# Gates, branch, output and down projections of an encoder layer in token-major form

## The chip, the core and the metric

One Trainium2 chip, one of its cores. The core has five engines with a queue each: TensorE (PE, with its weight loads shown as PEld), VectorE (DVE), ScalarE (ACT), GpSimd (POOL) and SyncE (SP), which here issues the transfers. The metric is device time of one execution in microseconds.

## What is computed

One layer for 256 tokens, `D_MODEL` 2048, all in float32. Cut to what the change touches:

```python
proj = h @ w_in                       # ..., the last 3 * 2048 columns are the gates
y_lru, y_attn, y_mem = ...            # recurrence, windowed attention, memory attention
gates = sigmoid(gl + b_gate).reshape(B, S, 3, D_MODEL)
merged = (gates[:, :, 0] * (y_lru @ w_br_lru) + gates[:, :, 1] * (y_attn @ w_br_attn)
          + gates[:, :, 2] * (y_mem @ w_br_mem))
x = x + rmsnorm(merged @ w_out, norm_mix_post)
hm = rmsnorm(x, norm_mlp_pre)
u = square(relu(hm @ w_up))           # 8192 wide
x = x + rmsnorm(u @ w_down, norm_mlp_post)
```

## The kernel before

Every product is float32 made of three fp32r products: a value is split into a high part (`h`, a rounded copy made by ACT) and a low part (the rest, made by DVE), and high x high, high x low and low x high are summed in PSUM. Weights come from DRAM as 344 chunks of 1 MB, each in two halves. `part` (line 106) issues a half's transfer on SP, lets ACT make `wh` and DVE make `wl`; `ahead` does this for the next chunk after each chunk's matmuls and then runs one step of every waiting list (`later`, `tick`). Five raw halves and four split halves have buffers. A scheduler sets the final order within each engine's queue; each queue runs in that order.

There are two forms of a product. In the **feature-major** form (`proj`, line 143) a chunk holds 128 output features for all 2048 inputs: the weights are the stationary operand, and the activations, high and low side by side, move: 16 matmuls of 512 columns with `wh` and 16 of 256 with `wl`. The result has 128 features on the partitions and its two halves are added on the way out (`ysum`, line 211: ACT copies one half, DVE adds the other, POOL multiplies by the norm's factor where one is given). `proj_one` (line 178) does the same with 48 matmuls of 256 columns into one half; `quad` (line 155) takes four chunks cut along the inputs and makes four results at once, so that it can begin when the first activations are there. In the **token-major** form (`proj_tok`, line 195) four chunks cut along the inputs make 512 features for two halves of 128 tokens: the activations are stationary and the weights move, 24 matmuls of 512 columns a chunk, and the result has tokens on the partitions. Before, this form serves the values of both attentions only.

The stages in order: the recurrence in four groups (`lru_group`), each with `quad` or `proj_one` chunks and, in the first three, gate chunks of the first branch behind it; keys, values and queries of the attention; the last gates, then the three branch products (`branch`, line 842) with the next gates or the memory attention between them; w_out; the norm, the residual `x1` and the split `h2` of the normed residual; `quad` for the first four w_up results; w_up and w_down in turn, four times. Gates get the norm's factor from POOL and bias and sigmoid from ACT; a branch result is multiplied and added by POOL. After w_out, squares are summed by POOL over the feature tiles, and `rstd_now` (line 358) sums over the partitions with small matmuls, takes the root, and spreads the factor over the partitions with another matmul; `warm` issues ten matmuls whose result nobody reads. All elementwise pages come from one pool of 31 pages of 4 KB for a partition.

## Time and profile before

| | us |
|---|---|
| median of three runs | 2093.64 (2091.84 to 2093.82) |
| profiled execution | 2091.72 |
| its span | 2089.9 |
| TensorE busy in it | 2032.9 |
| VectorE, ScalarE, GpSimd busy | 1358.2, 1081.8, 574.0 |

The span is from the first to the last instruction of the program; the execution's own time is 1.8 us longer. TensorE's matmuls overlap, so a matmul's length is longer than the distance to the next one: distances of starts tell the pace.

### The profile page before, as it was taken

The numbers are of one execution on the slowest core, as the hardware profiler recorded it, in microseconds if no ns is written. First come the engines' busy times: TensorE is split into PE (matmuls) and PEld (weight loads), VectorE is DVE, ScalarE is ACT, GpSimd is POOL, SyncE is SP. The second block draws the span as 40 slices with busy tenths as digits, with TensorE's granted clock in tenths as the row PEclk, the third lists the DMA queues.
The fourth block names the chain that finished last, engine by engine and source line by source line (L and its number), as shares of the span: only waits on it lengthen the run. The fifth ranks groups of instructions, "written<-read, shape, count | busy, mean of one in ns | idle before, by whom it ended". The sixth has DMA issues, their size and how long they took to land. (4 is left out here: it accounts for less than half of the span.)

```text
span 2089.9 us, 31160 instructions
## 1 busy us (share of the span) xinstructions
PE 2032.9 (97%) x12092; PEld 1811.8 (87%) x12092; DVE 1358.2 (65%) x1687; ACT 1081.8 (52%) x1607; POOL 574.0 (27%) x538
## 2 busy tenths in 40 slices
PE   8999999899999999999999999989999999999996
PEld 7999889799888888888888888878888888888886
DVE  8986685887557665555655555686556556555665
ACT  5877767567445454444454444444444444444442
POOL 5224141641116431000102237721001111111176
PEclk9999999999999999999999999999999999999998
DMA  6554546454566655555555556345555655556552
GB/s 228 189 184 148 190 157 201 152 169 144 183 196 206 202 187 176 181 172 175 179 171 183 190 199 218 128 165 188 192 189 184 194 189 186 195 184 191 191 187 96
DMA packets 108613, 378.25 MB, mean 181 GB/s; under 512 B 12720, under 2 KB 16816, under 8 KB 108464
## 3 DMA queue, kind: packets, MB, share of 16 engines
q1 hardware_dynamic: 108464, 376.26, 54.6%
q8 instruction: 94, 1.54, 0.3%
q14 instruction: 55, 0.45, 0.1%
HBM read 371.49 MB, written 2.10 MB: 179 GB/s over the span
## 5 line engine op out<-in xcount | busy, mean ns | idle before, releaser
L113 DVE TENSOR_TENSOR wl<-raw,wh 128x1024 fp32r<-128x1024 f32 (+1 forms) x691 | 897.1, 1301 | 234.8 <-ACT wh L112 228.1
L112 ACT ACTIVATE wh<-raw 128x1024 fp32r<-128x1024 f32 (+1 forms) x691 | 723.2, 1050 | 156.3 <-PE ps L137 58.6
L213 ACT ACTIVATE evac<-ps 128x256 f32<-128x256 f32 x294 | 112.2, 383 | 577.4 <-PE ps L137 574.1
L137 PE MATMUL ps<-hm,wh 128*128 128x512 f32 x1344 | 336.3, 393 | 0.0
L137 PEld LDWEIGHTS ps<-hm,wh 128*128 128x128 f32 x1344 | 244.6, 189 | 45.1
L137 PE MATMUL ps<-u,wh 128*128 128x512 f32 x1008 | 241.1, 391 | 0.0
L137 PE MATMUL ps<-h,wh 128*128 128x512 f32 x960 | 229.9, 391 | 0.0
L137 PEld LDWEIGHTS ps<-u,wh 128*128 128x128 f32 x1008 | 185.3, 188 | 35.8
L137 PEld LDWEIGHTS ps<-h,wh 128*128 128x128 f32 x960 | 176.4, 188 | 34.2
L141 PEld LDWEIGHTS ps<-hm,wl 128*128 128x128 f32 x1344 | 173.1, 192 | 12.0 <-DVE wl L113 5.4
L141 PE MATMUL ps<-hm,wl 128*128 128x256 f32 x1344 | 175.4, 283 | 5.2 <-DVE wl L113 5.2
L216 POOL TENSOR_TENSOR y<-y,rstd 128x256 f32<-128x256 f32 x64 | 49.1, 768 | 393.5 <-DVE y L214 372.9
L214 DVE TENSOR_TENSOR y<-ps,evac 128x256 f32<-128x256 f32 x111 | 47.0, 424 | 157.1 <-ACT evac L213 157.1
L189 PE MATMUL ps<-hm,wl 128*128 128x256 f32 x448 | 129.4, 289 | 11.9 <-DVE wl L113 11.9
L141 PEld LDWEIGHTS ps<-u,wl 128*128 128x128 f32 x1008 | 129.3, 191 | 4.9
L141 PE MATMUL ps<-u,wl 128*128 128x256 f32 x1008 | 130.8, 283 | 0.0
L187 PE MATMUL ps<-hm,wh 128*128 128x256 f32 x448 | 128.4, 287 | 1.0 <-ACT wh L112 1.0
L188 PE MATMUL ps<-hm,wh 128*128 128x256 f32 x448 | 128.0, 286 | 0.0
L141 PEld LDWEIGHTS ps<-h,wl 128*128 128x128 f32 x960 | 123.1, 191 | 4.7
L141 PE MATMUL ps<-h,wl 128*128 128x256 f32 x960 | 124.5, 283 | 0.0
L216 POOL TENSOR_TENSOR gate<-gate,rstd 128x256 f32<-128x256 f32 x48 | 43.0, 896 | 248.5 <-DVE gate L214 233.0
L189 PEld LDWEIGHTS ps<-hm,wl 128*128 128x128 f32 x448 | 87.3, 195 | 13.8 <-DVE wl L113 13.8
(283 smaller groups left out, 3084.5 us busy)
## 6 DMA issues: line engine op xcount, KB each, us to landing
raw<-wall SPq DMA_DIRECT2D x687, 512.0 KB, 3.5
raw<-wgate SPq DMA_DIRECT2D x8, 512.0 KB, 4.3
swap<-ry SPq DMA_DIRECT2D x40, 64.0 KB, 2.4
mp<-memT SPq DMA_DIRECT2D x4, 512.0 KB, 4.9
x<-xT SPq DMA_DIRECT2D x4, 512.0 KB, 4.6
xp<-xT SPq DMA_DIRECT2D x7, 256.0 KB, 6.9
out<-x SPq DMA_DIRECT2D x6, 256.0 KB, 2.3
raw<-wall SPq DMA_DIRECT2D x4, 128.0 KB, 2.5
```

The source lines that it names most:

```text
L112: nc.scalar.activation(hi[:, s], raw[:, s], AF.Copy)
L113: nc.vector.tensor_tensor(lo[:, s], raw[:, s], hi[:, s].bitcast(F32), op=ALU.subtract)
L137: self.nc.tensor.matmul(ps, wh, act[k // 2][:, k % 2, :], start=(k == 0), stop=(k == KT - 1))
L141: self.nc.tensor.matmul(ps[:, S:], wl, act[k // 2][:, k % 2, :S], start=False, stop=False)
L187: nc.tensor.matmul(o, wh, a[:, :S], start=(k == 0), stop=False)
L188: nc.tensor.matmul(o, wh, a[:, S:], start=False, stop=False)
L189: nc.tensor.matmul(o, wl, a[:, :S], start=False, stop=(k == KT - 1))
L213: self.nc.scalar.activation(t, ps[:, S:2 * S], AF.Copy)
L214: self.nc.vector.tensor_tensor(out, ps[:, :S], t, op=ALU.add)
L216: self.nc.gpsimd.tensor_tensor(out, out, r, op=ALU.mult)
```

## The change

The gates, the three branches, w_out and w_down now use the token-major form, so `merged`, `z`, `x1` and `z2` hold tokens on the partitions, four tiles of 512 features. `tok_mms` is the new inner part of `proj_tok`, which goes through half a chunk at a time: first all matmuls with `wh`, then those with `wl`. `proj_tok_late` does the last group of w_out and of w_down: its last two chunks run for the first 128 tokens, then for the second 128, and `after` is called for each. The norm's factor is one number for each partition now: ACT squares with a sum along the row (`squares`), `token_rstd` adds four sums, takes root and reciprocal, and the factor goes into one DVE operation with the residual (`scalar_tensor_tensor`). Gate biases and post-norm gains come as rows copied to all partitions. `w_up` stays feature-major, so the merged rows and the residual are transposed by TensorE (`turned`, `feed`): eight groups of four 128x128 transposes each. `feed` stands inside `quad`, two pairs of input tiles ahead. `rxcol`, the factor for each token, is made in the first group. `warm` behind w_out is gone. The attention's mask and its identity are fp32r tiles instead of bf16.

```diff
-    def proj_tok(self, act, specs):
...
-                for t in range(2):
-                    xh = a[:, t * P:(t + 1) * P]
-                    xl = a[:, S + t * P:S + (t + 1) * P]
-                    nc.tensor.matmul(pst[t], xh, wh, start=(k == 0), stop=False)
-                    nc.tensor.matmul(pst[t], xh, wl, start=False, stop=False)
-                    nc.tensor.matmul(pst[t], xl, wh, start=False, stop=(k == KT - 1))
+    def tok_mms(self, pst, act, ci, w, ts):
...
+        for half in range(2):
...
+            for i, k in enumerate(ks):
+                for t in ts:
+                    xh, xl = xs[k, t]
+                    nc.tensor.matmul(pst[t], xh, wh[i], start=(k == 0), stop=False)
+                    nc.tensor.matmul(pst[t], xl, wh[i], start=False, stop=False)
+            for i, k in enumerate(ks):
+                for t in ts:
+                    nc.tensor.matmul(pst[t], xs[k, t][0], wl[i], start=False, stop=(k == KT - 1))
+    def proj_tok_late(self, act, specs, after):
...
+        pair = [self.chunk(spec) for spec in specs[2:]]
+        for t in range(2):
+            for i in range(2):
+                self.tok_mms(pst, act, 2 + i, pair[i], (t,))
+            if t:
+                self.ahead()
+            after(t, pst[t])
+    def token_rstd(self, ssq):
...
+        tot = self.small.tile([P, 1], F32, tag="tot", name="tot")
+        nc.vector.reduce_sum(tot, ssq, axis=AX.X)
+        nc.scalar.activation(tot, tot, AF.Sqrt, scale=1.0 / D, bias=self.eps[:, 0:1])
+        nc.vector.reciprocal(tot, tot)
...
+    def squares(self, src, acc):
+        junk = self.tmp.tile([P, 2, S], F32, tag="pr", name="junk", bufs=3)
+        self.nc.scalar.activation(junk.rearrange("p a b -> p (a b)"), src, AF.Square, accum_out=acc)
+    def transposed(self, srcs, base):
...
+        tp = self.psc.tile([P, 2, S], F32, tag="sc", name="ft")
+        for t in range(2):
+            for kt in range(2):
+                at = base + kt * P
+                nc.tensor.transpose(tp[:, kt, t * P:(t + 1) * P], srcs[t][:, at:at + P], self.ident)
...
-                nc.tensor.matmul(far, self.identb, self.masks[t], start=False, stop=False)
+                nc.tensor.matmul(far, self.identr, self.masks[t], start=False, stop=False)
@@ gates_ahead @@
-                    self.gate(j, n, hm, held[n])
+            b = self.bias_tile(j, n)
+            pst = self.proj_tok(hm, [("T", "w_in", 9216 + j * D + n * 512, c) for c in range(4)])
...
+            for t in range(2):
+                nc.vector.scalar_tensor_tensor(g[:, t, :], pst[t], self.rxcol[:, t:t + 1], b, op0=ALU.mult, op1=ALU.add)
@@ branch @@
-        ps = self.proj(y, ("F", wname, n * P))
...
-        self.ysum(ps, t)
...
-            nc.gpsimd.tensor_tensor(t, t, g, op=ALU.mult)
-            nc.gpsimd.tensor_tensor(out, t, prev, op=ALU.add)
+        pst = self.proj_tok(y, [("T", wname, n * 512, c) for c in range(4)])
+        for t in range(2):
+            nc.vector.tensor_tensor(g[:, t, :], pst[t], g[:, t, :], op=ALU.mult)
+        if total is not None:
+            nc.vector.tensor_tensor(total, total, g, op=ALU.add)
@@ run, w_out to w_up @@
-                ps = self.proj(mg, ("F", "w_out", n * P))
-                self.ysum(ps, o)
-                self.square_into(acc, o, n == 0)
-                nc.gpsimd.tensor_scalar(o, o, gcol, None, op0=ALU.mult)
...
-        rp, r = self.rstd_now([acc, last])
-        self.warm(10)
+                self.squares(ps, ssq[:, t, n:n + 1])
+                nc.vector.tensor_tensor(z[n][:, t, :], ps, gains[n // 2][:, n % 2, :], op=ALU.mult)
...
+        def last_z(t, ps):
+            z_done(3)(t, ps)
...
+            rows.append(self.token_rstd(ssq[:, t, :]))
+            if t == 0:
+                for n in range(4):
+                    x1_part(0, rows[0], n, slice(0, 512))
...
+        def feed(p):
...
+            n, i = divmod(p, 2)
+            x1_part(1, rows[1], n, slice(2 * i * P, 2 * (i + 1) * P))
+            tp = self.transposed([x1[n][:, t, :] for t in range(2)], 2 * i * P)
...
+            for k in (2 * p, 2 * p + 1):
+                self.scaled_split(tp[:, k % 2, :], self.v("norm_mlp_pre", k), *self.hl(h2, k))
...
+        ups = self.quad(h2, [("T", "w_up", 0, c) for c in range(4)], feed)
@@ run, w_down @@
-                    self.ysum(self.proj(u, ("D", q, n * P)), t)
-                    nc.gpsimd.tensor_tensor(o, o, t, op=ALU.add)
...
+                        nc.vector.tensor_tensor(o, ps, o, op=ALU.add)
...
+                        self.squares(o, ssq[:, t, n:n + 1])
+                        nc.vector.tensor_tensor(o, o, gains[n // 2][:, n % 2, :], op=ALU.mult)
...
+            def last_z2(t, ps):
+                z2_done(3)(t, ps)
...
+                r = self.token_rstd(ssq[:, t, :])
+                for n in range(4):
...
+                    nc.vector.scalar_tensor_tensor(x, o, r, x, op0=ALU.mult, op1=ALU.add)
+                    nc.sync.dma_start(self.io["out"][:, t, n * 512:(n + 1) * 512], x)
```

What this does to the order, at three places. **TensorE, from the last w_up chunk to the first w_down chunk.** `ps` and `pst` are PSUM results, `h2` the normed residual, `u` the squared activations, `wh` and `wl` the weights' parts; numbers count tiles. Before:

```order
L137 MATMUL ps_14194<-h2_13358,wh_14179 128x512 x2
L137 MATMUL ps_14248<-u_13577,wh_14227 128x512 x2
L137 MATMUL ps_14248<-u_13594,wh_14227 128x512 x2
L137 MATMUL ps_14248<-u_13656,wh_14227 128x512 x2
L137 MATMUL ps_14248<-u_13763,wh_14227 128x512 x2
L141 MATMUL ps_14248<-u_13577,wl_14228 128x256 x2
L141 MATMUL ps_14248<-u_13594,wl_14228 128x256 x2
```

Now:

```order
L139 MATMUL ps_12770<-h2_12037,wh_12755 128x512 x2
L207 MATMUL pst_12824<-wh_12803,u_12153 128x512
L208 MATMUL pst_12824<-wh_12803,u_12153 128x512
L207 MATMUL pst_12825<-wh_12803,u_12153 128x512
L208 MATMUL pst_12825<-wh_12803,u_12153 128x512
L207 MATMUL pst_12824<-wh_12803,u_12153 128x512
L208 MATMUL pst_12824<-wh_12803,u_12153 128x512
L207 MATMUL pst_12825<-wh_12803,u_12153 128x512
L208 MATMUL pst_12825<-wh_12803,u_12153 128x512
L211 MATMUL pst_12824<-wl_12804,u_12153 128x512
L211 MATMUL pst_12825<-wl_12804,u_12153 128x512
L211 MATMUL pst_12824<-wl_12804,u_12153 128x512
```

The w_down chunk had 16 matmuls of 512 columns and 16 of 256; half a chunk now has eight with `wh` and four with `wl`, all of 512 and two of them for each token half and input tile.

**VectorE, from the norm behind w_out into `quad`.** `wl` are weight parts for w_up, `x` the residual, `h` the low part of the normed residual. Before:

```order
L113 TENSOR_TENSOR wl<-raw,wh 128x1024 x3
L933 TENSOR_SCALAR z<-ps,vec 128x256
L367 RECIPROCAL rcol<-rcol 128x2
L371 TENSOR_SCALAR diag<-ident,rcol 128x128 x2
L948 TENSOR_TENSOR z<-z,rb 128x256 x2
L949 TENSOR_TENSOR x_12421<-x_12421,z 128x256 x2
L952 TENSOR_TENSOR x_12421<-x_12421,z 128x512
L412 SCALAR_TENSOR_TENSOR h_13301<-x_12421,vec,h_13301 128x256 x2
...
L412 SCALAR_TENSOR_TENSOR h_13358<-x_13052,vec,h_13358 128x256 x2
L113 TENSOR_TENSOR wl<-raw,wh 128x1024 x4
```

Now:

```order
L965 SCALAR_TENSOR_TENSOR x_11679<-z,tot,x_11679 128x512
L115 TENSOR_TENSOR wl<-raw,wh 128x1024
L961 TENSOR_TENSOR z<-pst,gain 128x512
L385 TENSOR_REDUCE tot<-ssq 128x1
L115 TENSOR_TENSOR wl<-raw,wh 128x1024
L387 RECIPROCAL tot<-tot 128x1
L115 TENSOR_TENSOR wl<-raw,wh 128x1024
L965 SCALAR_TENSOR_TENSOR x_11198<-z,tot,x_11198 128x256 x2
L965 SCALAR_TENSOR_TENSOR x_11369<-z,tot,x_11369 128x256 x2
L965 SCALAR_TENSOR_TENSOR x_11524<-z,tot,x_11524 128x256 x2
L440 SCALAR_TENSOR_TENSOR h_11852<-ft,vec,h_11852 128x256
```

The weight parts stood behind all 16 splits; now three stand between the last token half's gain multiply and its residual, and the later ones between splits.

**VectorE, the end.** `z` is the result of w_down, `x` the residual that is written out. Before:

```order
L214 TENSOR_TENSOR y<-ps,evac 128x256
L998 TENSOR_TENSOR z_14826<-ps,z_14826 128x256
L999 TENSOR_TENSOR last<-z_14826 128x256
L367 RECIPROCAL rcol<-rcol 128x2
L371 TENSOR_SCALAR diag<-ident,rcol 128x128 x2
L1005 TENSOR_TENSOR z_14247<-z_14247,rb 128x256 x2
L1006 TENSOR_TENSOR x_12421<-x_12421,z_14247 128x256 x2
```

Now:

```order
L1048 SCALAR_TENSOR_TENSOR x_11679<-z_13270,tot,x_11679 128x512
L1035 TENSOR_TENSOR z_13270<-pst,z_13270 128x512
L1038 TENSOR_TENSOR z_13270<-z_13270,gain 128x512
L385 TENSOR_REDUCE tot<-ssq 128x1
L387 RECIPROCAL tot<-tot 128x1
L1048 SCALAR_TENSOR_TENSOR x_11198<-z_12823,tot,x_11198 128x512
L1048 SCALAR_TENSOR_TENSOR x_11369<-z_12972,tot,x_11369 128x512
L1048 SCALAR_TENSOR_TENSOR x_11524<-z_13121,tot,x_11524 128x512
L1048 SCALAR_TENSOR_TENSOR x_11679<-z_13270,tot,x_11679 128x512
```

Eleven multiplications and eleven additions of 256 columns on DVE, with five more of each on POOL, have become four operations of 512 columns for each token half; the first half's stand ahead of the second half's sum.

## Rows read from the trace of the kernel before

**Rows 1.** The page, part 1: busy us, share of the span, instructions.
```profile
PE 2032.9 (97%) x12092; PEld 1811.8 (87%) x12092; DVE 1358.2 (65%) x1687; ACT 1081.8 (52%) x1607; POOL 574.0 (27%) x538
```

**Rows 2.** By stage, busy us: PE, PEld, DVE, ACT, POOL; clock; DMA; GB/s.
```profile
40.00:330.00 290.00, 277.05 (x2018) 263.70 (x2017) 233.37 (x316) 207.83 (x294) 86.86 (x58) 0.99 0.53 177
...
520.00:1335.10 815.10, 814.83 (x4649) 717.70 (x4648) 480.74 (x527) 389.01 (x554) 219.59 (x201) 1.00 0.57 188
1335.10:1381.20 46.10, 33.98 (x167) 29.38 (x167) 40.66 (x49) 19.54 (x32) 22.64 (x21) 0.81 0.27 96
1381.20:2071.90 690.70, 690.70 (x3986) 611.06 (x3985) 410.15 (x499) 313.18 (x434) 140.00 (x155) 1.00 0.56 184
2071.90:2090.00 18.10, 1.81 (x12) 1.24 (x10) 12.22 (x27) 0.65 (x2) 9.14 (x11) 0.60 0.32 117
```

**Rows 3.** TensorE timeline, two w_up chunks: start, length (us), line, operands, count.
```profile
1396.31 3.82 PE L137 MATMUL ps<-h,wh 128*128 128x512 f32 x16
...
1401.88 3.82 PE L137 MATMUL ps<-h,wh 128*128 128x512 f32 x16
```

**Rows 4.** The same view, a token-major chunk: first matmul, what follows.
```profile
821.29 0.39 PE L205 MATMUL pst<-wh,mn 128*128 128x512 f32 x1
...
826.73 0.28 PE L792 MATMUL msc<-mk,qm 128*128 128x256 f32 x1
```

**Rows 5.** Instructions on tile mvh: count, least/middle/greatest ns, first and last start.
```profile
L732 ACT ACTIVATE mvh<-pst,rmcol x8: 677/684/692, 847.6 to 1066.0; 128x512 fp32r<-128x512 f32 x8
L733 DVE SCALAR_TENSOR_TENSOR mvl<-pst,rmcol,mvh x8: 740/742/743, 849.0 to 1067.5; 128x512 fp32r<-128x512 f32 x8
```

**Rows 6.** TensorE timeline, attention: four transposes, then scores with their mask.
```profile
409.26 0.60 PE L709 MATMUL tp<-ident,pr 128*128 128x128 f32 x4
409.62 0.36 PE L749 MATMUL sc<-kact,qa 128*128 128x256 f32 x1
409.82 0.23 PE L750 MATMUL sc<-mask,identb 128*128 128x128 bf16 x1
409.86 0.36 PE L751 MATMUL sc<-kact,qa 128*128 128x256 f32 x1
410.06 0.28 PE L752 MATMUL sc<-kact,qa 128*128 128x256 f32 x1
```

**Rows 7.** TensorE's waits, 40 to 330 us: total, times, longest.
```profile
PE ps L189 <- DVE wl L113: 11.9, 9, 2.9
```

**Rows 8.** TensorE timeline, w_out to w_up; last, a stretch as in rows 2.
```profile
1335.16 0.28 PE L363 MATMUL bc<-ones,zacc 128*128 128x1 f32 x2
...
1339.93 4.47 PE L389 MATMUL warm<-ones 128*128 128x128 f32 x20
1344.67 1.39 PE L167 MATMUL ps<-h,wh 128*128 128x512 f32 x4 [0.27 <-DVE h L412]
...
1366.73 1.22 PE L172 MATMUL ps<-h,wl 128*128 128x256 f32 x4 [8.31 <-DVE wl L113]
...
1381.23 2.20 PE L137 MATMUL ps<-h,wh 128*128 128x512 f32 x8
...
1366.70:1372.00 5.30, 5.27 (x16) 4.52 (x17) 5.30 (x6) 1.06 (x1) 0.00 (x0) 0.50 0.74 245
```

**Rows 9.** Groups by line: busy us, mean ns, idle before; last as rows 5.
```profile
L113 DVE TENSOR_TENSOR wl<-raw,wh 128x1024 fp32r<-128x1024 f32 x687 | 895.5, 1306 | 234.5 <-ACT wh L112 227.9
...
L977 DVE SCALAR_TENSOR_TENSOR y<-y 128x256 f32<-128x256 f32 x64 | 28.7, 451 | 50.0 <-POOL y L216 50.0
...
L412 DVE SCALAR_TENSOR_TENSOR h<-x,vec,h x16: 471/955/1482, 1343.7 to 1365.1; 128x256 fp32r<-128x256 f32 x16
```

**Rows 10.** Timeline of the end: `proj_one` from 2066.15, and the last transfer.
```profile
2066.15 0.28 PE L187 MATMUL ps<-u,wh 128*128 128x256 f32 x1
...
2071.90 0.28 PE L363 MATMUL bc<-ones,oacc 128*128 128x1 f32 x2
...
2086.88 0.33 SPq L1010 DMA_DIRECT2D out<-x  x1
```

More of the change, by code (lines that the diff above doesn't have):

```diff
@@ L826, in open_gate @@
         def open_gate(n):
-            return lambda: nc.scalar.activation(held[n], held[n], AF.Sigmoid, bias=self.v("b_gate", 16 * j + n))
-        def go(count=1):
-            for _ in range(count):
-                n = len(held)
-                if n < KT:
-                    if n % 4 == 0:
-                        pages.append(self.page_fp("gate"))
-                    held.append(pages[-1][:, n % 4, :])
-                    self.gate(j, n, hm, held[n])
-                    if at_once:
-                        self.later([], [open_gate(n)])
+            return lambda: nc.scalar.activation(held[n], held[n], AF.Sigmoid)
@@ L854, in startup, with turned, go, run @@
+    def turned(self, m, mg):
+        def go(i):
+            def run():
+                tp = self.transposed([m[:, t, :] for t in range(2)], 2 * i * P)
+                pg = self.page_act("mg")
+                mg.append(pg)
+                self.split(tp, pg[:, :, :S], pg[:, :, S:])
+            return run
+        return [go(0)], [go(1)]
     def startup(self):
         self.setup_rest()
-        self.later([self.rates], *self.rotary_tasks())
+        self.later([self.tokens_of_rx], [self.rates], *self.rotary_tasks())
@@ L893, in run @@
         self.later(*self.mem_tasks(mn))
-        for n in range(KT):
-            self.branch(1, "w_br_attn", n, yattn, gate1.held[n], merged[n], merged[n])
+        for n in range(4):
+            self.branch("w_br_attn", n, yattn, gate1.held[n], merged[n])
             gate1()
@@ L900, in run @@
             self.mem_head(h, hm, mn, ymem)
-        next_gate = self.gates_ahead(2, hm)
-        for _ in range(6):
-            next_gate()
+        gate2 = self.gates_ahead(2, hm)
+        gate2()
+        gate2()
         self.drain()
         mg = []
-        for n in range(KT):
-            m = merged[n]
-            self.branch(2, "w_br_mem", n, ymem, next_gate.held[n], m, m)
-            next_gate()
-            if n % 2 == 0:
-                mg.append(self.page_act("mg"))
-            self.split(m, *self.hl(mg, n))
@@ L956, in run @@
-        ups = self.quad(h2, [("T", "w_up", 0, c) for c in range(4)])
-        for i in range(8):
-            s = slice(2 * (i % 2), 2 * (i % 2) + 2)
-            x = x1[i // 2][:, s, :]
-            if i < 4:
-                self.pair_sq(nc.gpsimd, accs, "p", x)
-            else:
-                self.pair_sq(nc.vector, accs, "d", x)
-        r2 = self.pair_rstd(accs, "ra")
-        z2 = []
-        acc = self.tmp.tile([P, S], F32, tag="sqacc", name="oacc", bufs=1)
+        for n in range(4):
+            self.branch("w_br_mem", n, ymem, gate2.held[n], merged[n])
+            self.later(*self.turned(merged[n], mg))
+            gate2()
@@ new lines, in run, with z_done, go, x1_part @@
+        z, x1, ssq = [], [], self.small.tile([P, 2, 4], F32, tag="ssq", name="ssq")
+        gains = [self.page_tok("gain") for _ in range(2)]
+        for i in range(2):
+            nc.sync.dma_start(gains[i], self.io["gmix"][:, 2 * i:2 * i + 2, :])
+        def z_done(n):
+            def go(t, ps):
+                self.squares(ps, ssq[:, t, n:n + 1])
+                nc.vector.tensor_tensor(z[n][:, t, :], ps, gains[n // 2][:, n % 2, :], op=ALU.mult)
+            return go
+        def x1_part(t, r, n, s):
+            nc.vector.scalar_tensor_tensor(x1[n][:, t, s], z[n][:, t, s], r, x1[n][:, t, s], op0=ALU.mult, op1=ALU.add)
```

229 lines of the change are left out of this document (111 added, 118 removed).

## The prediction

> **What bounds the kernel now.** I read the page's busy shares first: TensorE 97% of the span against 65% for VectorE [rows 1]. Then the span cut by stage [rows 2]: in 520 to 1335 us and in 1381 to 2072 us TensorE stands still for 0.3 us and for nothing, at full granted clock. There the time is a count of matmuls by their pitch. Where the change reaches, it loses time in three places: in the recurrent stage (13 us of 40 to 330), between w_out and w_up (46.1 us at a granted clock of 0.81), and after the last matmul (18.1 us). So I price the change as a pitch, and then those three places one by one.
>
> **The pitch.** A feature-major chunk (`proj`: 16 matmuls of 512 columns, 16 of 256) starts 5.57 us after the one ahead of it [rows 3]. A token-major chunk of the same 1 MB of weights (24 matmuls of 512) takes 826.73 - 821.29 = 5.44 us [rows 4], or 227 ns for each matmul. Both stream 12,288 columns; 512 columns at 2.4 GHz are 213 ns, so each matmul carries some 13 ns of its own, and the token form has 8 fewer. The change turns 48 gate, 48 branch, 16 out and 64 down chunks, 176 in all. Two of them were `proj_one`, 48 matmuls of 256 columns, 2071.90 - 2066.15 = 5.75 us [rows 10]. Gain: 174 x 0.127 + 2 x 0.31 = **22.7 us**. The new order within a chunk (four matmuls of `wh` twice the length of those of `wl`, as before, but all `wh` of two k first) changes neither their number nor their length; where the old order needs `wl` 0.23 us into a half, the new one needs it 1.8 us in, as late as `proj` does, so I put nothing there.
>
> The Trainium skill (TensorE: Matmul & The Clock Gate, section Back-to-back issue gap) gives N/2.4 + 2.5 ns for an isolated warm matmul. By that a feature chunk would be an estimated 5.20 us, a token chunk 5.18, and the gain 3.7 us instead of 22.7. The two measured chunks [rows 3, 4] contradict it, by 227 ns where it has 216, so the sum goes by the rows.
>
> **Evacuations and queues.** Four gate or branch chunks had four ACT copies, four DVE adds and four to eight POOL operations; now two DVE operations of 128x512 follow each group of four. The like of them, on the result of a token group, took 742 ns, with 684 ns for ACT's [rows 5]. 2 x 0.74 = 1.5 us in 21.8 us is nothing that TensorE sees: the two banks of the group have four banks behind them, and the weight parts for the next chunk stand ahead of them on DVE. Their cover is DVE's slack: 481 of 815 us busy in that stage [rows 2]. The added transfers (12 biases, 4 gains; x1 is as large as before) stand in SP's queue with the weights. In the built order each bias waits for a DVE operation that comes before the one the next weight transfer waits for; gains and x1 wait for TensorE or POOL work that is done hundreds of matmuls before the next weights are used. Price zero; if one were held, the next weights would be late by as much.
>
> **Transposes.** `merged` is turned in 8 groups of four. Four transposes of the attention took 409.62 - 409.26 = 0.36 us, and the matmul behind them came 0.08 us later than its like [rows 6]: 8 x 0.44 = **3.5 us added**.
>
> **Masks.** A bf16 mask matmul takes 0.04 us and the fp32r one behind it 0.20 instead of 0.12 [rows 6]: 0.12 us for the two together, 32 times. An fp32r one of 128 columns isn't in the trace. Between 0.04 (the bf16 one) and 0.227 (a matmul of 512) the whole is -2.6 to +3.4 us. It is nearest to the 256-column one, 0.12: I enter 0.
>
> **Between w_out and w_up.** Before: last w_out matmul ends 1335.16, first matmul of the quad 1344.67, a stall of 8.3 us for `wl`, which the order has behind all 16 splits on DVE, 5.3 us at half the clock (1.2 GHz) behind it, first plain w_up chunk 1381.23 [rows 8]. That is 46.1 us for 64 x 0.227 + 64 x 0.120 = 22.2 us of matmuls. After, token half 0 is finished 24 matmuls (5.4 us) before half 1, but the order shows what stands on DVE between the last matmul and the first quad matmul: the tail of half 0's four 512-wide updates (two of four), a weight part, the gain multiply, the sum, two more weight parts, six x1 updates, a split. With 0.74 for 512 wide [rows 5], 1.31 for a part, 0.45 for 256 wide, and 0.47 for a split with no POOL beside it (its least; the middle is 0.96) [rows 9]: about 1.4 + 1.3 + 0.7 + 0.2 + 2.6 + 2.7 + 0.5 = 9.4 us. The head is as long as before. What goes is the 8.3 us stall, since weight parts now alternate with splits. What comes: 6 groups of transposes inside the quad (6 x 0.44 = 2.6 us), a wait for a split here and there (about 1 us), and the clock: TensorE has idled some 6 us with no `warm` matmuls, and after 8.3 us of idling 5.3 us ran at half rate [rows 8], so 2 us lost. 9.5 + 22.2 + 2.6 + 1 + 2 = 37.3: **gain 9 us**. Ends: 29 us if half 1's chain overtakes the weight parts (gain 17), 57 us if the whole quad ran at 1.2 GHz (loss 11). I stay near the middle, which each engine's own work supports: DVE has some 28 us there, too.
>
> **The tail.** Before, 18.1 us [rows 2] from the last matmul to the end, with 3.0 us from the last issue at 2086.88 to the end of the span [rows 10]. After, half 0's chain starts 5.4 us earlier and takes about 6 us of DVE, so half 1 starts some 0.8 us late. Then add 0.74, square 0.68, gain multiply 0.74 [rows 5], sum, root and reciprocal 0.8 with handovers, four updates of 0.74, transfer 3.0: 9.8 us. **Gain 8.3 us**; ends 6 (a transfer of 256 KB lands later) and 9.5.
>
> **Recurrent stage.** TensorE waited 11.9 us for `wl` there [rows 7], always in `proj_one` chunks, which the change leaves. Gate evacuations are two DVE operations of 512 columns instead of four of 256, and POOL has less to do beside DVE. I enter 0, ends -6 and +6.
>
> **Sum:** -22.7 + 3.5 + 0 - 9 - 8.3 + 0 = -36.5 us. The profiled execution took 2091.72 us (span 2089.9): 2055.2. It lies 1.9 us under the median of the three runs, about as far as those lie apart, so I predict **2055 us**.
>
> **Rivals.** (a) The forecast, with its terms' ends partly added: 2047 to 2064. (b) The extra 13 ns doesn't go with the number of matmuls: if in the new order, which changes the moving tile and the bank more often, a matmul took 232 ns, 24 of them would be a feature chunk; gain 0.6 instead of 22.7, time 2077. The rule of the skill named above would end near it, at an estimated 2074. Against it: both chunk lengths are measured, in this kernel. (c) The handover to w_up gives nothing back, since DVE's three weight parts and the lower clock fill it: 2064 to 2075. For it: my own head of 9.4 us; against it: the 8.3 us stall has no cause left. (d) The recurrent stage shifts by more than 6 us, since DVE is late there already and gate results arrive in bursts: 2062 to 2075, or under 2047 if the waits vanish with POOL's work. (e) **Slower than before:** DVE's two evacuations behind every group of four wait for its last matmul and hold the next weight part, and TensorE stands still at each of the 44 groups. One evacuation pair and a weight part on the path are 1.48 + 1.31 = 2.8 us [rows 5, 9], 123 us over all, so 2178; it decides from 36.5/44 = 0.83 us for a group. For it: it is how TensorE waits in the recurrent stage. Against it: five token groups of this shape are in the trace, and the stage that holds four of them has 0.3 us of waits [rows 2, 5].
>
> That the form isn't what is said is out: the built order has 24 matmuls of 512 columns for each turned chunk.
>
> **How the numbers follow.** (a) 0.72, (b) 0.07, (c) 0.10, (d) 0.07, (e) 0.04. The range 2045 to 2066 holds (a) but for 0.02, most of (c) and half of (d). A measurement can tell about 0.2%, or 4 us, from no change; only (e) ends over 2098, and 0.01 is left for something between: faster 0.95, same 0.01, slower 0.04.
>
> **What would show it.** Right: token chunks 5.44 us apart in gates, branches and w_down; 35 to 39 us between the last w_out matmul and the first plain w_up chunk, with a granted clock under 1 in it; some 10 us after the last matmul; waits of TensorE for `wl` in the recurrent stage near 12 us. Wrong: a pitch over 230 ns, a new group of waits for `wl` or `pst` outside the recurrent stage, or a handover of 45 us.

## The result, and the profile after

The changed kernel takes 2058.47 us (median of four runs, 2057.77 to 2058.98) against 2093.52 us before: a ratio of 0.9834, 95% interval 0.9817 to 0.9851. The forecast was 2055 us with a range of 2045 to 2066. The profiled execution took 2058.98 us, its span 2057.2; against the profiled one of before (2091.72) that is -32.7 us, where the sum said -36.5.

First the page's busy shares, which answer [rows 1]; then the stages as in [rows 2], with bounds at the same places of the program to half a microsecond.

```profile
PE 2009.2 (98%) x10670; PEld 1737.5 (84%) x10670; DVE 1286.0 (63%) x1588; ACT 1048.8 (51%) x1449; POOL 266.6 (13%) x241
```

```profile
41.30:334.90 293.60, 278.41 (x1922) 261.25 (x1921) 226.33 (x311) 209.48 (x277) 78.49 (x46) 0.98 0.54 176
525.00:1331.00 806.00, 806.00 (x3916) 681.06 (x3915) 458.46 (x483) 367.11 (x449) 46.94 (x47) 1.00 0.59 192
1331.00:1366.00 35.00, 28.45 (x163) 24.48 (x161) 25.26 (x47) 21.52 (x49) 0.00 (x0) 0.90 0.43 143
1366.00:2048.40 682.40, 682.40 (x3457) 583.34 (x3456) 390.14 (x472) 305.72 (x395) 49.31 (x64) 1.00 0.57 188
2048.40:2057.20 8.80, 0.01 (x1) 0.00 (x0) 4.41 (x9) 1.02 (x3) 0.00 (x0) 0.70 0.52 197
```

Both long stretches are still all matmuls at full clock, and shorter. The handover from w_out to w_up went from 46.1 to 35.0 us, the tail from 18.1 to 8.8 us. Of these stages only the recurrent one grew, from 290.0 to 293.6 us, although its token chunks are shorter and DVE and GpSimd are busy for less time than before: that is the line against the forecast. Part of it is idling, 293.60 - 278.41 = 15.2 us where TensorE idled 13.0 before [rows 2]; the rest is longer matmuls, for TensorE is busy 1.4 us longer where shorter chunks alone should have saved 1.5. The granted clock shows it: by the traces 13.7 us of this stage ran at 0.50 (1.2 GHz), and 6.8 before.

The pitch, on TensorE's timeline in w_down (start, length, line, operands, count). A chunk begins at the first row and the next at the last one: 1441.05 - 1435.61 = 5.44 us, as in [rows 4], with the new order inside.

```profile
1435.61 0.39 PE L207 MATMUL pst<-wh,u 128*128 128x512 f32 x1
...
1437.42 1.07 PE L211 MATMUL pst<-wl,u 128*128 128x512 f32 x4
...
1441.05 0.39 PE L207 MATMUL pst<-wh,u 128*128 128x512 f32 x1
```

The handover, same view, and one stretch of it by window. It answers [rows 8].

```profile
1330.36 0.62 PE L211 MATMUL pst<-wl,mg 128*128 128x512 f32 x2
1330.82 0.60 PE L411 MATMUL ft<-ident,x 128*128 128x128 f32 x4
1336.70 1.11 PE L411 MATMUL ft<-ident,x 128*128 128x128 f32 x4 [5.28 <-DVE x L965]
1339.07 2.07 PE L171 MATMUL ps<-h,wh 128*128 128x512 f32 x4 [1.26 <-DVE h L440]
...
1365.96 2.11 PE L139 MATMUL ps<-h,wh 128*128 128x512 f32 x8
```

```profile
1336.70:1342.00 5.30, 4.04 (x14) 3.15 (x14) 4.37 (x11) 4.61 (x14) 0.00 (x0) 0.50 0.47 162
```

Some 8.1 us from the end of w_out (1331.0) to the first quad matmul, 26.9 us for the quad. The 8.3 us stall of [rows 8] has nothing in its place. TensorE idles for 5.3 us, and the first 5.3 us behind that have a granted clock of 0.50 (1.2 GHz): 14 matmuls run at half rate.

The end: DVE's timeline around the last matmul, which answers [rows 10].

```profile
2047.81 0.74 DVE L1048 SCALAR_TENSOR_TENSOR x<-z,tot,x 128x512 f32<-128x512 f32 x1
2048.02 0.39 PE L211 MATMUL pst<-wl,u 128*128 128x512 f32 x1
2048.47 0.68 DVE L1035 TENSOR_TENSOR z<-pst,z 128x512 f32<-128x512 f32 x1
...
2050.00 0.69 DVE L1038 TENSOR_TENSOR z<-z,gain 128x512 f32<-128x512 f32 x1 [0.85 <-ACT junk L403]
...
2051.32 2.74 DVE L1048 SCALAR_TENSOR_TENSOR x<-z,tot,x 128x512 f32<-128x512 f32 x4
```

Half 0's four updates end as half 1's last matmul does, so half 1's chain starts at once: add, square, gain, sum, four updates, and 3.1 us for the last transfer.

In the recurrent stage TensorE's waits (total, times, longest), which answer [rows 7]:

```profile
PE ps L193 <- DVE wl L115: 13.7, 7, 2.9
PE pst L211 <- DVE wl L115: 0.9, 1, 0.9
```

### The profile page after: what moved, and what is told of

Same layout as the page of the kernel before. It is cut to its first block, busy times and chain, and to the rows that moved or that the text cites. A ratio compares the mean times of both kernels' runs of the same rounds, so it can differ in the third digit from the quotient of the medians.

```text
span 2057.2 us, 27735 instructions
## 1 busy us (share of the span) xinstructions
PE 2009.2 (98%) x10670; PEld 1737.5 (84%) x10670; DVE 1286.0 (63%) x1588; ACT 1048.8 (51%) x1449; POOL 266.6 (13%) x241
## 4 chain that ended last, share of the span: by engine, by line
PE 90%; DVE 6%; issue 1%; ACT 1%; POOL 1%; DMA 1%; SPq 0%; DVEq 0%; POOLq 0%; ACTq 0%
PE ps L139 19%; PE pst L208 17%; PE pst L207 17%; PE pst L211 17%; PE ps L143 10%; DVE wl L115 2%; PE ps L193 1%; PE ps L192 1%; PE ps L191 1%; PE ps L171 1%; DVE xc L523 1%; PE ps L176 1%; DVE ip L621 1%; PE tp L737 0%; PE av L749 0%
## 5 line engine op out<-in xcount | busy, mean ns | idle before, releaser
L207 PE MATMUL pst<-wh,u 128*128 128x512 f32 x512 | 199.2, 389 | 0.0
L208 PE MATMUL pst<-wh,u 128*128 128x512 f32 x512 | 199.2, 389 | 0.0
L207 PE MATMUL pst<-wh,hm 128*128 128x512 f32 x416 | 163.2, 392 | 0.0
L208 PE MATMUL pst<-wh,hm 128*128 128x512 f32 x416 | 162.4, 390 | 0.0
L235 ACT ACTIVATE evac<-ps 128x256 f32<-128x256 f32 x120 | 45.4, 382 | 215.1 <-PE ps L139 210.5
L193 PE MATMUL ps<-hm,wl 128*128 128x256 f32 x448 | 130.5, 291 | 13.7 <-DVE wl L115 13.7
L139 PE MATMUL ps<-hm,wh 128*128 128x512 f32 x576 | 143.8, 394 | 0.0
L211 PE MATMUL pst<-wl,u 128*128 128x512 f32 x512 | 137.5, 389 | 0.0
L139 PEld LDWEIGHTS ps<-hm,wh 128*128 128x128 f32 x576 | 104.9, 190 | 19.4
L208 PEld LDWEIGHTS pst<-wh,u 128*128 128x128 f32 x512 | 96.1, 188 | 20.0
L211 PEld LDWEIGHTS pst<-wl,u 128*128 128x128 f32 x512 | 96.1, 188 | 20.0
L207 PEld LDWEIGHTS pst<-wh,u 128*128 128x128 f32 x512 | 96.1, 188 | 19.9
L211 PE MATMUL pst<-wl,hm 128*128 128x512 f32 x416 | 111.4, 389 | 0.9 <-DVE wl L115 0.9
```

The source lines that it names most:

```text
L139: self.nc.tensor.matmul(ps, wh, act[k // 2][:, k % 2, :], start=(k == 0), stop=(k == KT - 1))
L193: nc.tensor.matmul(o, wl, a[:, :S], start=False, stop=(k == KT - 1))
L207: nc.tensor.matmul(pst[t], xh, wh[i], start=(k == 0), stop=False)
L208: nc.tensor.matmul(pst[t], xl, wh[i], start=False, stop=False)
L211: nc.tensor.matmul(pst[t], xs[k, t][0], wl[i], start=False, stop=(k == KT - 1))
L235: self.nc.scalar.activation(t, ps[:, S:2 * S], AF.Copy)
```

## The experiments

All start from the changed kernel. Runs 2, 3, 4, 9 and 10 put one part of it back, the others alter or add one thing, and run 11 joins several. Times are medians of four executions where nothing else is said, to be held against 2058.47 us; code is cut at "...".

**1. The pitch: twice as many matmuls for the same columns, in w_down.**

```
+cuts = [slice(0, 256), slice(256, 512)] if self.plan[-1][1] == "w_down" else [slice(0, 512)]
...
+def mm(o, x, r, **kw):
+    for s in cuts:
...
+        nc.tensor.matmul(o[:, s], x, r[:, s], start=first, stop=last)
...
-nc.tensor.matmul(pst[t], xh, wh[i], start=(k == 0), stop=False)
+mm(pst[t], xh, wh[i], start=(k == 0), stop=False)
```

> In w_down alone each matmul of 512 columns is cut into two of 256: 48 for a chunk in place of 24, the same columns and the same arithmetic. Pace theory (some 13 ns come with each matmul; a 256-column one has a pitch of 120 ns, a 512-column one 227): 48 x 0.120 = 5.76 us a chunk in place of 5.44, over 64 chunks +20 us, 2078.5 us. Rival (the gain of the token-major chunk came from fewer weight reads or from the order in the chunk, not from the count of matmuls): 5.44 us a chunk and 2058.5 us.

Measured: 2079.23 us (2078.28 to 2079.89), +20.8. TensorE's timeline, one chunk from the first row to the last, 5.76 us:

```profile
1454.74 2.08 PE L204 MATMUL pst<-wh,u 128*128 128x256 f32 x16
1456.66 1.12 PE L204 MATMUL pst<-wl,u 128*128 128x256 f32 x8
...
1460.50 2.08 PE L204 MATMUL pst<-wh,u 128*128 128x256 f32 x16
```

Columns and sums are the same; 24 more matmuls cost 0.32 us, 13 ns each. A cost that comes with each matmul is shown, and with it the largest term of the forecast. Every added matmul has a weight load of its own, though (PEld x12206 on this run's page, x10670 in the changed kernel), so the run doesn't tell the matmul's own part from its load's, and the weight reads that the rival names stay untested. The Trainium skill (TensorE: Matmul & The Clock Gate, section Back-to-back issue gap) has N/2.4 + 2.5 ns for an isolated warm matmul, from which 24 more matmuls would come to an estimated 0.06 us; the 0.32 us measured contradict that here.

**2. The order inside a token chunk, put back.**

```
 nc.tensor.matmul(pst[t], xh, wh[i], start=(k == 0), stop=False)
-nc.tensor.matmul(pst[t], xl, wh[i], start=False, stop=False)
...
-        nc.tensor.matmul(pst[t], xs[k, t][0], wl[i], start=False, stop=(k == KT - 1))
+nc.tensor.matmul(pst[t], xh, wl[i], start=False, stop=False)
+nc.tensor.matmul(pst[t], xl, wh[i], start=False, stop=(k == KT - 1))
```

> The token-major chunks get the order of the kernel before back (for each 128 input rows wh, wl, wh), where the change puts the 8 matmuls of a half with wh ahead of the 4 with wl. Same matmuls. Theory (the gain of a chunk is its count of matmuls; the order only gives slack to wl): the pitch of token-major chunks stays 5.44 us, nothing changes from branch 0 on, and the gates of the recurrent stage wait 1 to 3 us more for wl: 2058.5 to 2062. Rival (the order carries the gain): token chunks go to 5.57 us, 174 x 0.13 = 22 us, 2080 us.

Measured: 2061.1 us (2060.88 to 2063.92), +2.6. The rival is out: the four chunks of the first memory value product take 25.02 us in all three kernels, and branch and w_down chunks keep their length. Token chunks up to the values `v` now wait for `wl` 3.6 us where they waited 0.9:

```profile
PE ps L193 <- DVE wl L115: 10.5, 7, 2.9
PE pst L208 <- DVE wl L115: 3.6, 2, 2.7
```

So the order gives slack where DVE is late, and changes nothing in the branches and w_down.

**3. The recurrent stage: gate 0 put back to feature-major.**

```
+if j == 0:                      # gates_ahead
...
+    for i in range(4):
+        ps = self.proj(hm, ("F", "w_in", 9216 + (4 * n + i) * P))
+        self.ysum(ps, page[:, i, :], self.rx)
+    return
```

The gate values that come out are not the layer's; instructions and sizes are.

> Gate 0 alone goes back to feature-major chunks (its 16 chunks, an evacuation of three operations each, a sigmoid for each 128 features); all else is the changed kernel. Its rows then lie otherwise than the branch's, and its bias is another column: the sums are not the block's, the instructions and sizes are. Pace theory: 16 chunks at 5.57 us in place of 5.44, +2.0 us. Theory A (the recurrent stage lost 5 us because gate 0 moved): the stage between the end of the first quad and the end of v comes back to the 286.9 us of before from 290.4 (that is the pace's +1.5 and -5.1 of stalls), together about 2055.5 us. Rival B (the shift of the rotary tasks by one tick or the start of the kernel made the loss, gate 0 is innocent): the stage keeps its stalls and gets 1.5 us longer, 2060.5 us.

Measured: 2060.05 us (2058.29 to 2061.06). The stretch from the first chunk behind the first quad to the values `v` is 289.8 us, where theory A had 286.9 and the changed kernel 290.5. Less the 1.5 us of pitch, 2.2 us of the 5.1 that were lost came back. TensorE's waits there:

```profile
PE ps L193 <- DVE wl L115: 11.9, 10, 2.4
PE ps L143 <- DVE wl L115: 1.6, 2, 1.4
```

As the owner of the whole loss, gate 0 is out: with it back the sum of waits is nearly the same, cut into more pieces at other places, and TensorE idles 14.7 us there (15.2 in the changed kernel). Most of the 2.2 us is clock: 6.8 us of the stretch at 0.50 in place of 13.7. The theory has its point in one place, though: the four xr chunks of the third group (input of the recurrence) take 24.6 us here, 24.2 before, 28.6 in the changed kernel.

**4. The recurrent stage: the tasks of the rotary tables back to their step.**

```
-self.later([self.tokens_of_rx], [self.rates], *self.rotary_tasks())
+self.later([self.tokens_of_rx, self.rates], *self.rotary_tasks())
```

> The transposes that bring 1/rms of x to one value per token are issued in the same step as the rates, as was the step of the rates before, so that the rates and the rotary tasks come one chunk earlier, where they stood in the kernel before. Theory C (the recurrent stage's 12 us of waits fall where the order on DVE and ACT happens to put the weight parts; no single part of the change owns the loss): the stage stays within 2 us of the changed kernel's, 2056.5 to 2060.5. Rival B (the shift by one chunk made the loss): the stage is 4 us shorter, 2054 to 2055.

Measured: 2058.12 us (2057.56 to 2059.3), no change. Rival B falls. The waits are longer in sum (15.2 us in ten pieces), and lie elsewhere again: the third group's four xr chunks are back at 24.3 us, the second group's gl chunks (gate of the recurrence) lost 3.6.

**5. The recurrent stage: ACT's order.** The third group shows how the time is lost. ACT's, GpSimd's and DVE's timeline of the changed kernel, at the end of the second group's work:

```profile
173.42 1.28 ACT L588 ACT_TABLE_LOAD   x1
175.24 1.28 ACT L573 ACT_TABLE_LOAD   x1
...
179.86 1.28 ACT L588 ACT_TABLE_LOAD   x1
...
189.07 2.42 POOL L611 TENSOR_TENSOR ip<-ip,T 128x1024 f32<-128x1024 f32 x1
...
191.53 0.69 DVE L621 TENSOR_TENSOR_SCAN ip<-rp,ip 128x256 f32<-128x256 f32 x1 [3.00 <-POOL ip L611]
```

ACT switches its table for one exponential (173.42), back for four sigmoids (175.24), and again (179.86). The first scan (the recurrence's running sum, on DVE) starts at 191.53, 8.6 us after TensorE began the third group at 182.88. The same view of before, where that group began at 182.14:

```profile
184.24 2.39 POOL L583 TENSOR_TENSOR ip<-ip,T 128x1024 f32<-128x1024 f32 x1
...
186.67 0.69 DVE L593 TENSOR_TENSOR_SCAN ip<-rp,ip 128x256 f32<-128x256 f32 x1 [3.21 <-POOL ip L583]
```

There it was 4.5 us. Four microseconds later the scans and convolutions stand on DVE ahead of the weight parts that the group's middle chunks want. The other traces bear this out: wherever `proj_one` has the changed kernel's order, the group's four xr chunks take 24.2 to 24.6 us with a first scan 4.5 to 5.9 us after the group's start (before, runs 3 and 4), and 28.1 to 28.6 us with one 8.6 to 11.9 us after it (runs 1, 2 and 7 to 10). The test holds the exponentials of the first three groups (the recurrence's decays, which the scans need) back until the group's last sigmoid:

```
+col = box["dec"][:, at:at + 1] if g < 3 else self.rate[:, 1, at:at + 1]
+nc.scalar.activation(rp[d][:, b, :], rp[d][:, b, :], AF.Exp, scale=col)
...
+def hold():
+    box["dec"] = self.dec
+    nc.vector.scalar_tensor_tensor(box["dec"], ip[1][:, 3, :32], 0.0, self.rate[:, 1, :], op0=ALU.mult, op1=ALU.add)
...
-[rate(0, 3), rate(1, 3), inject(1, 0)],
+[rate(0, 3), rate(1, 3), hold, inject(1, 0)],
```

> The exponentials of the decays in the first three recurrent groups are held back until the group's last sigmoid, by one small DVE instruction that copies the rate columns and reads the last sigmoid's output; the ACT stream then has 37 table loads in place of 54 (1.28 us each in the trace). Theory A (the changed order on ACT, with one more pair of table loads in a group, brings the decays out 5 us later, so that the scans fall on the weight parts of the third group's chunks): the decays end some 4 to 8 us earlier, TensorE's waits for wl in the recurrent stage fall below the 11.9 us of before, and the kernel comes to 2052 to 2056 us. Rival (the two evacuations of a gate group, which come in one piece on DVE, hold the weight parts): no change beyond 1 us, 2057.5 to 2059.5.

Measured: 2054.62 us (2053.62 to 2055.37), -3.9. In its trace:

```profile
187.78 0.69 DVE L627 TENSOR_TENSOR_SCAN ip<-rp,ip 128x256 f32<-128x256 f32 x1 [3.01 <-POOL ip L617]
```

```profile
40.02:327.60 287.58, 274.55 (x1908) 258.20 (x1907) 231.27 (x315) 186.06 (x259) 76.23 (x46) 0.98 0.55 181
```

The group begins at 183.25, the scan 4.5 us later, and its four xr chunks take 24.2 us, as before the change. The time is as theory A has it, the size of the waits is not: 12.3 us in sum, not under 11.9. The second view is the stretch of run 3, the first chunk behind the first quad to `v`: 2.9 us shorter than the changed kernel's 290.5, with 2.2 us less idling (13.0 us, as much as before the change). Of the 3.7 us by which the span is shorter another 0.9 lies in the first quad, whose code is the same. The edit takes loads out of all three groups, 17 in number, so it doesn't weigh the one pair alone.

**6. The recurrent stage: TensorE's order.**

```
 for k in range(KT):             # proj_one
...
     nc.tensor.matmul(o, wh, a[:, :S], start=(k == 0), stop=False)
     nc.tensor.matmul(o, wh, a[:, S:], start=False, stop=False)
-    nc.tensor.matmul(o, wl, a[:, :S], start=False, stop=(k == KT - 1))
+for k in range(KT):
+    wl = w[k // 8][1][:, (k % 8) * P:(k % 8 + 1) * P]
+    nc.tensor.matmul(o, wl, act[k // 2][:, k % 2, :S], start=False, stop=(k == KT - 1))
```

> In the feature-major chunks of the recurrent stage (the groups of xr and gl after the first, 28 chunks) TensorE takes the 32 matmuls with wh first and the 16 with wl last, where it took wl in every third place: wl is wanted 3.84 us into a chunk (32 x 0.12) and no longer 0.24 us into it. Same matmuls, same sums. Theory (the seven waits for wl there, 13.7 us, are parts that DVE delivers 1 to 3 us too late for this order, and each also costs some clock afterwards): TensorE's waits for wl in these chunks fall below 4 us and the kernel comes to 2046 to 2050 us. Rival (DVE is what limits the stage, and a wait only moves to a later chunk): the waits stay above 10 us in sum, 2056 to 2060 us.

Measured: 2055.5 us (2053.63 to 2057.47), -3.0, just outside the rival's range. TensorE's waits, and the stretch of run 3 in this kernel:

```profile
PE ps L195 <- DVE wl L115: 7.9, 6, 2.4
PE ps L191 <- ACT wh L114: 4.6, 2, 3.4
```

```profile
39.68:325.92 286.24, 272.35 (x1909) 255.99 (x1907) 226.02 (x308) 205.80 (x275) 78.16 (x46) 0.99 0.55 180
```

The waits for `wl` fell by 5.8 us, those for `wh` rose by 3.9: more slack for the one part uncovers the other. On waits the rival is nearer: TensorE idles 13.9 us, only 1.3 less than in the changed kernel. The stretch is 4.2 us shorter all the same, since its matmuls take 2.9 us less: 6.8 us of it have the lower clock and no longer 13.7.

**7. The handover: feeds ahead of the quad.**

```
-feed(0)
-feed(1)
-ups = self.quad(h2, [("T", "w_up", 0, c) for c in range(4)], feed)
+for p in range(8):
+    feed(p)
+ups = self.quad(h2, [("T", "w_up", 0, c) for c in range(4)])
```

> All eight feeds (x1 of token half 1, transposes, the split of h2) stand ahead of the first w_up group and none inside it. Theory: the weight parts of that group pass DVE only between feeds; with the feeds ahead, TensorE starts the group some 7 us later (8 feeds of about 1.2 us on DVE, two of which lie ahead of it now), runs more of it at the low clock, and the stretch from the last w_out matmul to the first plain w_up chunk goes from 35 us to 41 to 44: 2065 to 2068 us. Rival (the 8.3 us stall of before went only because POOL's multiplications no longer hold DVE, so the interleaving is worth nothing): within 1.5 us, 2057 to 2060.

Measured: 2058.45 us (2057.4 to 2059.51), no change; the quad took 27.9 us, +1.0. DVE's order of splits and weight parts hardly differs from the changed kernel's, since the scheduler alternates them in either form. So this run shows that their place in the code is worth 1 us at most. It leaves the alternation untested, and doesn't tell why the stall went.

**8. The handover: GpSimd's work put back as a load.**

```
+for i in range(12):             # ahead of feed(0)
+    self.pair_sq(nc.gpsimd, load, "p", x1[i % 4][:, 0, :]...)
```

> Added work, nothing taken away: 12 rounds of squares on GpSimd over x1's rows of token half 0 (23 instructions, about 1.25 us each by the rows of before, 29 us), whose result nobody reads, issued when the handover from w_out to w_up begins. Theory (in the kernel before, the splits of h took 0.99 us on DVE in place of 0.48 while GpSimd worked, and that held the weight parts behind them: the 8.3 us stall went because GpSimd has nothing to do there any more): the splits go back to some 0.9 us and the stretch from the last w_out matmul to the first plain w_up chunk grows by 8 to 14 us, 2066 to 2072 us. Rival (the stall went for another reason, such as the order that the instructions have now): at most 1 us, 2058 to 2060.

Measured: 2067.74 us (2066.19 to 2069.61), +9.3. The size is the theory's, the place isn't. DVE's groups by form, 1328 to 1373 us (count, busy us, mean ns), first of the changed kernel, then with the load:

```profile
L115 DVE TENSOR_TENSOR wl<-raw,wh 128x1024 fp32r<-128x1024 f32 x13 | 15.9, 1222 | 6.5 <-ACT wh L114 6.5
L440 DVE SCALAR_TENSOR_TENSOR h<-ft,vec,h 128x256 fp32r<-128x256 f32 x16 | 7.3, 480 | 3.6 <-ACT h L439 3.5
L965 DVE SCALAR_TENSOR_TENSOR x<-z,tot,x 128x256 f32<-128x256 f32 x8 | 3.3, 480 | 0.0
```

```profile
L115 DVE TENSOR_TENSOR wl<-raw,wh 128x1024 fp32r<-128x1024 f32 x10 | 14.7, 1470 | 6.2 <-ACT wh L114 6.2
L965 DVE SCALAR_TENSOR_TENSOR x<-z,tot,x 128x256 f32<-128x256 f32 x8 | 9.7, 1273 | 0.0
L440 DVE SCALAR_TENSOR_TENSOR h<-ft,vec,h 128x256 fp32r<-128x256 f32 x16 | 7.3, 478 | 3.1 <-ACT h L439 3.0
```

The updates of x go from 480 to 1273 ns and hold the first transposes 9.9 us, where they held 5.3; the first quad matmul comes 17.3 us after w_out, where it came after 8.1. The splits stay at 478 ns. In the kernel before they took 955 ns in the mean [rows 9]; there their source was x in SBUF, now it is the transposed tile `ft` in PSUM. So the change took GpSimd's work away and also moved the splits out of its reach. Sixteen splits at 0.48 us more than now are 7.6 us, an estimate from [rows 9] that is near the 8.3 us of the stall; no run puts GpSimd's work beside splits that read SBUF, so that this made the stall is argued, not shown. The Trainium skill (SBUF — State Buffer, section Who interferes with whom) says that a DVE instruction with two inputs in SBUF contends with a GpSimd instruction that reads SBUF, that one with a single SBUF input doesn't (outside certain faster modes), and that the order of issue decides which of the two is blocked. The rows agree: x reads z and x from SBUF, h reads `ft` from PSUM and only its high part from SBUF.

**9. Both ends: token half 0 not finished early.**

```
-self.proj_tok_late(mg, specs, last_z)     # and w_down likewise
+pst = self.proj_tok(mg, specs)
+for t in range(2): last_z(t, pst[t])
```

> The last group of w_out and of w_down runs both token halves chunk by chunk as the others do, in place of finishing token half 0 two half-chunks (5.4 us) earlier. Theory (the finish of half 0 hidden beside half 1's matmuls is what shortened both ends): after the last matmul there is half 0's work too, 4 to 4.5 us of DVE at each end, so 2065 to 2068 us. Rival (the shorter chains of column sums are what shortened the ends, and the halves overlap each other anyway): at most 1.5 us at each end, 2059 to 2061.5.

Measured: 2062.34 us (2061.85 to 2063.57), +3.9: 1.1 us at the handover, 2.7 at the end, nearer to the rival. DVE's timeline of the end: the last group's two halves stand behind each other.

```profile
2050.09 1.29 DVE L1036 TENSOR_TENSOR z<-pst,z 128x512 f32<-128x512 f32 x2 [9.24 <-PE pst L211]
...
2053.03 2.74 DVE L1049 SCALAR_TENSOR_TENSOR x<-z,tot,x 128x512 f32<-128x512 f32 x4
...
2055.88 2.74 DVE L1049 SCALAR_TENSOR_TENSOR x<-z,tot,x 128x512 f32<-128x512 f32 x4
```

Of the 9.2 us that the tail gained, 2.7 are the early half; the other 6.5 are what is left by subtraction, and go with the shorter chain (sums along the free axis, no column sums on TensorE, updates in one pass); no run takes these apart.

**10. Masks back in bf16.**

```
-matmul(far, self.identr, self.masks[t])   # fp32r
+matmul(far, self.identb, self.masks[t])   # bf16
```

> Masks and the identity that they are multiplied with go back to bf16; all else is the changed kernel. By the traces of the two kernels the pair of the mask's matmul and the one behind it takes 241 ns with bf16 and 229 ns with fp32r, 32 times: +0.4 us, which is within what two runs of one kernel differ by, 2057.5 to 2060. Rival (the casts of the masks on DVE made the start or the recurrent stage longer): 2055 to 2057.

Measured: 2057.63 us (2056.87 to 2060.01): no difference that can be told. In the trace of the changed kernel the mask and the matmul behind it take 415.71 - 415.49 = 0.22 us (0.24 in [rows 6]):

```profile
415.49 0.22 PE L778 MATMUL sc<-mask,identr 128*128 128x128 f32 x1
415.54 0.33 PE L779 MATMUL sc<-kact,qa 128*128 128x256 f32 x1
415.71 0.28 PE L780 MATMUL sc<-kact,qa 128*128 128x256 f32 x1
```

**11. Together.** The held exponentials, the order with `wh` first, and the last gain at the end on GpSimd:

```
-nc.vector.tensor_tensor(o, o, gains[n // 2][:, n % 2, :], op=ALU.mult)
+eng = nc.gpsimd if n == 3 else nc.vector
+eng.tensor_tensor(o, o, gains[n // 2][:, n % 2, :], op=ALU.mult)
```

> The held-back exponentials and the order with wh first together, and at the very end the gain of the last column group multiplied on GpSimd instead of on DVE (0.69 us that stood ahead of the sum there). If the two work on different waits they add: 2058.5 - 3.9 - 3.0 - 0.7 = 2051 us. If both take away the same waits for wl, the larger counts alone: 2054 us.

Measured: 2052.17 us (2050.62 to 2054.04), -6.3: the parts overlap a little. Waits for `wl` in recurrent chunks are at 7.6 us and the tail at 8.5. Then also the forward product of the last recurrent group on DVE (`drive`, 128x1024):

> The same, and in the last recurrent group the product ahead of the forward scans runs on DVE (about 1.2 us) and not on GpSimd (3.4 us). Theory (the stall of 4.8 us at 379 to 384 us in every kernel so far is a scan that stands on DVE ahead of two weight parts and waits for GpSimd's product): that stall goes, -3 to -5 us against the combined kernel. Rival (the parts are late there for DVE's load, not for the waiting scan): within 1 us of it.

Measured: 2050.41 us (five runs, 2049.94 to 2054.59), ratio to the kernel before 0.979, interval 0.9777 to 0.9803. It is the fastest of all here and lies 8.1 us below the changed kernel, but the 1.8 us to the run above are inside the spread of either. The single wait that it aimed at went from 4.7 to 2.8 us, the sum of that kind only from 5.8 to 5.4: the theory of the waiting scan isn't settled.

## Why the prediction was right, and which term was off

| term | predicted | measured in the trace |
|---|---|---|
| pitch, 176 chunks, by the chunk's 5.44 us | -22.7 | -22.7 |
| transposes of merged | +3.5 | +3.8 |
| masks | 0 | -0.4 |
| w_out to w_up | -9 | -11.1 |
| tail | -8.3 | -9.2 |
| recurrent stage, idling and clock | 0 | +5.1 |
| start and attention (not in the sum) | 0 | +1.3, +0.4 |
| a wait of before at w_out (not in the sum) | 0 | -0.3 |
| sum | -36.5 | -32.7 |

The masks' 0.4 us is part of the attention's line and not added again. That line goes from `v` to the second branch; in it stands one wait for `wl` that the kernel before hasn't, 1.27 us at 405.50. The last line but one is a wait of 0.3 us for `mg` that is gone.

**The pitch** held to the hundredth: 5.44 us a chunk, and run 1 shows that it goes with the count of matmuls and their weight loads. (Redone, the gain by the rule that the forecast cites is 3.6 us, not 3.7; nothing hangs on it.) That also disposes of rival (b), and with the two long stretches without a wait, of (e): two DVE operations behind each token group hold nothing.

**Transposes.** TensorE's timeline at the first group:

```profile
1136.61 0.60 PE L411 MATMUL ft<-ident,gate 128*128 128x128 f32 x4
1136.96 0.48 PE L207 MATMUL pst<-wh,hm 128*128 128x512 f32 x1
1137.27 0.40 PE L208 MATMUL pst<-wh,hm 128*128 128x512 f32 x1
```

The four take 0.35 us, and the matmul behind them 0.31 where 0.23 is usual: the 0.08 us for the change of type is there, as priced. The 32 chunks of branch 2 and the gates beside them took 180.0 us instead of 181.2; by their pitch alone they would have gained 4.1, so the six groups among them cost 2.9, or 0.48 each. The other two stand in w_out, and eight make 3.8.

**The handover.** Right in kind: the stall went, the head stayed (8.1 us for 9.5), and the clock cost at most the 2 us that were priced, half of the 4.04 us that TensorE worked at 0.50 [rows 8]. It is 2 us better than forecast, a bit more than half of it in the head; the rest is that quad and transposes took 26.9 us where 27.8 were entered. The reason given for the stall's end, that parts now alternate with splits, no run tests, for run 7 left the alternation as it was. Run 8 points to another that the forecast didn't have: GpSimd has nothing to do there, and the splits read PSUM. Rival (c) had its head of 9.4 us nearly right and its conclusion wrong.

**The tail.** The forecast has half 1 start 0.8 us late behind half 0. The rows of the end show that it isn't late at all, and that is the difference of 1 us.

**The recurrent stage is the term that was mis-sized**: 0 entered, ends -6 and +6, +5.1 measured, the shorter chunks taken out, with 13.7 us of waits for the "near 12" that the text wanted to see, and a granted clock of 0.98 for 0.99. TensorE's added idling is 2.2 us of it, and 2.9 are matmuls that ran longer at the lower clock, for which the forecast had no term here. Of the five other profiles with the same code up to this stage's end (run 10 but for the masks' casts) run 1 has the same length, and runs 7 to 10 have 1.2 to 1.4 us less, so the loss lies between 4 and 5. The step that failed is that the waits come "always in `proj_one` chunks, which the change leaves": the chunks were left, the order on ACT and DVE around them wasn't. The scheduler placed one more pair of table loads into a group, the scans came 4 us later against the chunks, and DVE did them ahead of weight parts. Late scans go with late parts in every trace with this order of TensorE (run 5), and run 5's edit takes the idling back to that of before; how much of it the one pair of loads made stays open, since the edit took out 17 loads. What is left after it, 287.6 us against the 285.4 that pitch alone would give, is matmul time at the lower clock. That gate 0's form, or the shift of the rotary tasks, owned the whole loss is refuted by runs 3 and 4: each moved the waits, and neither made them go. What stays is a stage in which DVE delivers parts just in time, and in which any new order shifts where TensorE waits, for 11 to 16 us in sum (by TensorE's idle time in that stretch of the traces). The clock then adds its part: behind the wait in the chunk that begins at 223 us the granted clock is 0.50 for 5.5 us, 28 matmuls at 1.2 GHz.

```profile
227.00:232.50 5.50, 5.50 (x28) 5.50 (x27) 5.50 (x8) 3.21 (x4) 0.00 (x0) 0.50 0.72 223
```

Why the scheduler chose this order was not looked into.

The start (+1.3 us) can't be put down to the change: over the changed kernel and the twelve built from it the first quad takes between 34.95 and 37.26 us, with the same code up to its end but for run 10's masks. The kernel before, with one trace, had 34.85.

The forecast lay 3.5 us under the median. It is the recurrent stage's 5 us and 2 at the start, in the attention and from the transposes, against 3 us more than forecast from the handover and the tail. That these errors half cancel is luck; the large term, the pitch, is not.

## What to carry to other kernels

With fixed columns, count the matmuls: each carries, with its weight load, a cost of its own (13 ns here), so a layout with fewer and wider ones gains by a number that two chunks of the old trace already give. Where a scheduler sets the order, an edit isn't free in a stage that runs just in time, even if it takes work out of it; look for its table loads and for long operations ahead of the parts that TensorE waits for, before a gain there is entered as zero, and add what the lower clock takes behind each new wait. And ask of every DVE instruction near GpSimd's work where its operands lie.

## What was not expected of the hardware

A DVE instruction can stand still while a GpSimd instruction runs. In the changed kernel a convolution step that takes 0.46 us elsewhere took 2.63 us, and ended with GpSimd's sum of 128x1024 (219.07 + 4.49 = 223.56):

```profile
219.07 4.49 POOL L625 TENSOR_TENSOR ip<-ip 128x1024 f32<-128x1024 f32 x1 [9.72 <-DVE ip L621]
...
221.21 2.63 DVE L523 SCALAR_TENSOR_TENSOR xc<-xr,vec,xc 128x255 f32<-128x255 f32 x1
```

That step reads xr and xc from SBUF and started second. It isn't as simple as that, though: three other DVE instructions with two inputs in SBUF (a weight part at 219.14, splits at 220.28 and 220.61) also started behind that sum by the trace and kept their lengths. The sum took 2.40 us at its least (400.16), so it was perhaps held first; no run shows that. The weight parts late in run 8, at 1352.37, 1355.84 and 1359.34, kept their 1.23 us beside GpSimd's work: each started 0.13 to 0.16 us ahead of a GpSimd instruction, and that took 1.96 to 1.99 in place of 1.10.

A 128-column fp32r matmul with its own weights, which [rows 6] could not show, takes 0.05 us, and the one behind it 0.17 instead of the 0.20 behind a bf16 one.
